# A hybrid decoder step on one core: a second buffer of values, rows' sums in the ring of general buffers, the state's chain over nine tenths of a pair's stretch, and the order at the program's two ends

## The chip, the cores and the metric

One core of a Trainium2 chip runs the whole program. The time is the device time of one execution in microseconds (us), the median of several; lower is better. In the profile the engines are PE (TensorE, matmuls), PEld (its weight loads), DVE (VectorE), ACT (ScalarE), POOL (GpSimd) and SP (SyncE, which issues nearly all DMAs).

## The reference

One layer of a hybrid decoder for a prompt of 2048 rows and 8 sequences of 4 new rows, all in float32 with a width of 1024. The normalised rows are multiplied by one large matrix; a short convolution, a recurrent state (RWKV-7, 16 heads of 64) and two gates work on its columns; two output projections are gated and added, a third follows, then a residual sum and a norm.

```python
h = _rmsnorm(x, norm_g)
p = jnp.einsum('bsd,dn->bsn', h, w_in)                 # 1024 x 10368 columns
...
y_c = bg * conv * jax.nn.silu(zc)                      # conv: 3 taps of cg * xin
...
# the state of a head, row after row:
S = (S * d_t[:, :, None, :] + sa[..., None] * (kk_t * a_t)[:, :, None, :]
     + v_t[..., None] * k_t[:, :, None, :])            # sa = S @ (-kk_t)
y = jnp.einsum('bhvk,bhk->bhv', S, r_t)
...
m = jax.nn.sigmoid(gc) * (y_c @ w_out_c) + jax.nn.sigmoid(gr) * (y_r @ w_out_r)
out = x + m @ w_o                                      # then the final _rmsnorm
```

The outputs are the normed rows and the new states of convolution, shift and recurrence.

## The kernel before

**Matrices in halves.** Every large product is made of float32 operands split into a high part and a low part (`fp32r`): a tile of rows stands in XH and XL, a tile of weights in whl[0] and whl[1], and three matmuls (high by high, low by high, high by low) give one product. Weights are read from HBM into `wraw`, ACT copies the high part (`w_advance`), DVE subtracts to get the low part (`w_lows`), and both halves are stored for later sets.

**Sets and pairs.** The 2048 rows are four sets of 512 (`th` 0 to 3; the last, LAST, has the 32 new rows as well), and in each set the 16 heads are 8 pairs (`p`). The main stream of PE is the projections (`ip<-XH,whl`, `ip<-XL,whl`) of nine or ten column blocks per pair. Around it runs, as side jobs written as Python generators (`Side`, line 498), the recurrence in chunks of 64 rows: `rwkv_keys` (decays, keys), `rwkv_solve` and `rwkv_merge` (scores GM and the inverse of a triangular matrix, Xbd), `rwkv_load` (values into SV, transposed keys into BKt), `rwkv_chain` and `rwkv_out` (norm of the rows' sums Yc, output).

**The chain** (line 1362) is what is serial. For each of the 8 chunks of a pair: PE multiplies the state (`pa<-S,AR`), DVE adds into UB, PE multiplies (`pb<-UB,Xbd`), ACT copies the upper half of SV, PE multiplies (`pb<-SV,BKt`), DVE makes the new state S. The chain of pair k runs during the stretch of pair k+1.

**What sets the order.** While the program is recorded, a planner (`Clock`) keeps a time per engine. `begin_pair` (1761) and `run_pair` (1775) give each side job a piece of the pair's stretch by the shares in CUTS, and `drive` (552) lets a job take its next step when its share and the operands' planned readiness allow. PE's order is that in which it is recorded; DVE's and ACT's instructions are sorted by planned start at the end (1825). Engines take their instructions in order. A DMA is booked by `dma_start` (336) on SP's clock with its size over 290 bytes per ns.

**Buffers.** `tmp` (605) is a ring of 8 general tiles (`Ring`, 182); if none is free, side jobs are run ahead until one is. SV and Yc exist once, so `rwkv_load` of a pair waits for the chain of the pair before (it writes SV and BKt), and the chain waits for the `rwkv_out` before it. During sets 1 to 3 the job `comb` makes sums of quarters of the output matrices: `part_of` (1584) copies a high half into one of two tiles `qs` (ACT), subtracts the low half (DVE) and stores both (SP, 512 KB), 108 times.

**The two ends.** At the start `prep_first` (741) scales the first rows (kept in GM), transposes them on PE and makes XH and XL. At the end `out_phase` (2063) adds the last product of each quarter of 128 rows to its sum (`out_done`, 2022), squares it, and `finish` (2009) makes the root (DVE, POOL, DVE) and scales both halves of the rows, quarter after quarter.

In the trace nearly all instructions have line L264 and the DMAs L337: there the recording layer calls the engine. So tiles tell them apart.

Of the kernel before, what the change touches and what calls it, by code (L numbers as in the profile page):

```python
# [30 lines left out]
CUTS = {"most": (0.7, 0.0, 0.0, 0.34, 0.7, 0.95, 0.95), "last": (0.6, 0.3, 0.68, 0.4, 0.7, 0.97, 0.9),  # L31
# [313 lines left out]
def hybrid_kernel(tc, x_prompt, x_sample, state_conv, state_shift, state_rwkv, norm_g, w_in, conv_w,  # L345
# [61 lines left out]
    raws, parts_, lows = {}, {}, []  # L407
    state = {"use": 0, "dma": 0, "split": 0}

    def w_advance(dma, split, load):  # L410
        while state["dma"] < min(dma, len(order)):
            _, src, n, _, there = order[state["dma"]]
            if not there:
                raw = wraw_p.tile()
                SP.dma_start(out=raw.rearrange("p (kt n) -> p kt n", n=n),
                             in_=src.rearrange("(kt p) n -> p kt n", p=P))
                raws[state["dma"]] = raw
            state["dma"] += 1
        while state["split"] < len(order):
            i = state["split"]  # L420
            _, src, n, keep, there = order[i]
            if i >= (load if there else split):
                break
            hl = whl_p.tile([P, 2, NB * P], F32R, name="whl")
            if there:
                for c0, c1, part in keep if isinstance(keep, list) else [(0, NB * P, keep)]:
                    SP.dma_start(out=hl.bitcast(F32)[:, :, c0:c1], in_=part)
            else:
                raw = raws.pop(i)
                A.copy(hl[:, 0], raw)  # L430
                lows.append((hl, raw, keep))
            parts_[i] = tuple(hl[:, k].rearrange("p (kt n) -> p kt n", n=n) for k in range(2))
            state["split"] += 1

    def w_lows():
        while lows:
            hl, raw, keep = lows.pop(0)
            was, clock.kind = clock.kind, "low"
            V.tensor_tensor(out=hl[:, 1], in0=raw, in1=hl[:, 0].bitcast(F32), op=ALU.subtract)
# [165 lines left out]
    tmp = Ring(ph1.enter_context(tc.tile_pool(name="tmp", bufs=1)), [P, NT + 64], 8, clock)  # L605
# [17 lines left out]
    SV = xp.tile([P, NC1, P], F32, name="SV")  # L623
# [5 lines left out]
    def load_early(i):  # L629
# [3 lines left out]
        else:  # L633
            xt = (BKt if i == 2 else SV).rearrange("p a b -> p (a b)")[:, 0:D]
# [106 lines left out]
    def prep_first(half):  # L741
# [4 lines left out]
        for k, i in enumerate(ts):  # L746
            xt = early[i]
            sc = rstd[:, i:i + 1]
            if k % 2:
                A.activation(out=xt, in_=xt, func=AF.Copy, scale=sc)  # L750
            else:
                V.tensor_scalar(out=xt, in0=xt, scalar1=sc, scalar2=None, op0=ALU.mult)
# [548 lines left out]
    def rwkv_load(th, p, o):  # L1301

        vT = o["vT"]
        samp = th == LAST
# [6 lines left out]
        yield W["bt"], (), 1  # L1311
        for c0 in range(0, NCH + samp, 4):
# [4 lines left out]
            if c0 == NCH:  # L1317
                T.transpose(pt[:, P:2 * P], vT[:, NTT[th] - P:NTT[th]], ident)
                A.copy(SV[64:64 + NSAMP, NCH, :], pt[P - NSAMP:P, P:2 * P])
            A.copy(BKt[:, c0:c0 + k, :], pt[:, 0:k * P].rearrange("p (c x) -> p c x", x=P))  # L1320
            yield W["bt"], (), 1
        yield W["merge"], [SV[64:128], BKt]
# [31 lines left out]
    def all_rows(o, GM, Yc, samp):  # L1354

        o["left"] = o.get("left", 1 + samp) - 1
        if not o["left"]:
            own_rows(0, NCH, GM, Yc)
            if samp:
                own_rows(NCH, 1, GM, Yc)  # L1360

    def rwkv_chain(th, p, o):
# [4 lines left out]
        S = St[p]  # L1367
# [41 lines left out]
    def rwkv_sequences(th, p, o):  # L1409
# [64 lines left out]
        yield W["samp"], [SV[0:64, c, :]], 2  # L1474
        all_rows(o, GM, Yc, True)

    def rwkv_out(th, p, o):
# [24 lines left out]
        for c2 in range(2):  # L1502
            for h in range(2):
# [3 lines left out]
                             func=AF.Identity, scale=lw[HS[c2], p:p + 1], bias=lb[HS[c2], p:p + 1])  # L1507
        if samp:
# [239 lines left out]
    def zero_rest():  # L1748
        for t in (UP[64:128, 1].bitcast(F32), UP[0:64, 3].bitcast(F32), BK[:, NCH], ARB[0][:, NCH], ARB[1][:, NCH], *XB, *UB, SV[:, NCH]):
# [11 lines left out]
    def begin_pair(th, p, total):  # L1761
# [10 lines left out]
        job["load", k] = Side(rwkv_load(th, p, o), "load", [job["keys", k]] + read(k - 1)).over(f[4], f[5])  # L1772
        return o

    def run_pair(th, p, total, end):
# [4 lines left out]
        after = [prior("merge", k), prior("load", k), prior("out", k - 1)]  # L1780
# [228 lines left out]
    def finish(r, pieces, m=P):  # L2009

        ms, f, z = (nwt.tile([P, 1], F32, name=f"f{i}", bufs=2)[0:m] for i in range(3))
        V.scalar_tensor_tensor(out=ms, in0=fs[0:m, 1, r:r + 1], scalar=1.0 / D, in1=fs[0:m, 0, r:r + 1], op0=ALU.mult, op1=ALU.add)
        G.tensor_tensor(out=f, in0=ms, in1=mhalf[0:m], op=ALU.pow)
        V.scalar_tensor_tensor(out=z, in0=f, scalar=ms, in1=f, op0=ALU.mult, op1=ALU.mult)
# [5 lines left out]
        SP.store(d0, t0)  # L2020

# [41 lines left out]
    def out_phase(n):  # L2063
# [8 lines left out]
        if n == len(seq) - 1:  # L2072
# [108 lines left out]
```

## Time and profile before

| | us |
|---|---|
| median of 3 runs | 3046.71 (3045.75 to 3051.43) |
| profiled execution, whole | 3049.82 |
| its span, first to last instruction | 3048.1 |
| PE busy in the span | 2986.7 |
| DVE busy | 2162.2 |
| ACT busy | 1346.4 |
| mean granted clock of PE | 0.997 |

The difference of 1.7 us between the profiled execution and its span lies outside the first and last instruction. A matmul's end is modelled in the trace and overlaps the next one's start, so PE's busy time hides short delays; the distance from start to start tells them. A wait is named by what ended it.

### The profile page before, as it was taken

Reading aid. Unit: us, or ns where it says so; the run is one execution under the profiler, and the core shown is the slowest. Engines: PE = TensorE matmul, PEld = TensorE weight load, DVE = VectorE, ACT = ScalarE, POOL = GpSimd, SP = SyncE. Lnnn points to the kernel's source line nnn. Section 1 sums busy time; section 2 is a strip of 40 time slices with the busy share of each in tenths; the row PEclk is TensorE's granted clock in tenths of the full one; section 3 lists DMA queues with packets and bytes.
Section 4 is the critical chain, followed back from the end, with each engine's and each line's share of the span. In section 5 each row is a group of like instructions: output and inputs, shape, how many; then the busy total and the mean of one; then the engine's idle time right before and its main releaser. Section 6 shows DMA issues by size and latency. Waiting matters only on the chain. (4 is left out here: it accounts for less than half of the span.)

```text
span 3048.1 us, 56138 instructions
## 1 busy us (share of the span) xinstructions
PE 2986.7 (98%) x21370; PEld 2559.5 (84%) x21370; DVE 2162.2 (71%) x5504; ACT 1346.4 (44%) x2745; POOL 314.2 (10%) x520
## 2 busy tenths in 40 slices
PE   7999999999999999999999999999999999999998
PEld 6778777788887788788787899999999998888996
DVE  5777777767777777777777777667767744486675
ACT  5555554554444445444444444444444322424223
POOL 2011111111111111111111110000100000000000
PEclk9999999999999999999999999999999999999999
DMA  7877767766666667666665665444344589998775
GB/s 273 291 235 238 252 223 236 230 222 227 207 218 210 212 215 246 219 218 218 218 223 208 201 214 181 150 136 143 128 141 135 169 262 330 325 325 294 267 261 195
DMA packets 319731, 678.05 MB, mean 222 GB/s; under 512 B 47610, under 2 KB 179827, under 8 KB 269798
## 3 DMA queue, kind: packets, MB, share of 16 engines
q1 hardware_dynamic: 310758, 670.27, 65.0%
q10 hardware_dynamic: 8704, 4.20, 0.5%
q8 instruction: 169, 2.77, 0.4%
q14 instruction: 100, 0.82, 0.1%
HBM read 479.10 MB, written 195.28 MB: 221 GB/s over the span
## 5 line engine op out<-in xcount | busy, mean ns | idle before, releaser
L264 PE MATMUL ip<-XH,whl 128*128 128x512 f32 (+3 forms) x6832 | 1854.3, 351 | 4.6 <-DVE whl L264 3.8
L264 PEld LDWEIGHTS ip<-XH,whl 128*128 128x128 f32 x6832 | 1173.9, 189 | 136.3 <-issue 7.0
L264 PE MATMUL ip<-XL,whl 128*128 128x512 f32 (+3 forms) x3416 | 1195.7, 350 | 2.2 <-POOL XL L264 2.2
L264 PEld LDWEIGHTS ip<-XL,whl 128*128 128x128 f32 x3416 | 646.6, 189 | 67.8 <-issue 5.5
L264 DVE SCALAR_TENSOR_TENSOR S<-pb,pe,sp 64x64 f32<-64x64 f32 x512 | 143.3, 280 | 98.2 <-PE pb L264 91.4
L264 DVE TENSOR_TENSOR tt<-Mi,X 128x60 f32<-128x60 f32 (+21 forms) x864 | 190.3, 220 | 24.9
L264 DVE TENSOR_TENSOR X<-X,tt 128x60 f32<-128x60 f32 (+21 forms) x864 | 187.9, 217 | 27.9
L264 ACT ACTIVATE sp<-S,pe 128x128 f32<-128x128 f32 x256 | 102.4, 400 | 205.8 <-DVE S L264 203.5
L264 ACT COPY SV<-pb 64x128 f32<-64x128 f32 x256 | 66.1, 258 | 283.8 <-PE pb L264 279.5
L264 DVE TENSOR_TENSOR UB<-pa,P 64x64 f32<-64x64 f32 x512 | 110.3, 215 | 111.8 <-PE pa L264 88.8
L264 ACT ACTIVATE tmp<-ip,vec 128x512 f32<-128x512 f32 (+2 forms) x174 | 103.0, 593 | 182.6 <-PE ip L264 178.0
L264 PE MATMUL acc<-XH,whl 128*128 128x264 f32 (+1 forms) x800 | 141.2, 329 | 0.5 <-DVE tmp L264 0.5
L264 PEld LDWEIGHTS acc<-XH,whl 128*128 128x128 f32 x800 | 119.0, 188 | 14.9 <-DVE tmp L264 0.7
L264 PEld LDWEIGHTS pb<-UB,Xbd 128*128 128x128 f32 x512 | 85.0, 188 | 40.5 <-PE ip L264 16.1
L264 PE MATMUL acc<-UA,whl 128*128 128x264 f32 (+1 forms) x720 | 116.1, 321 | 1.0 <-DVE My L264 1.0
L264 DVE TENSOR_TENSOR whl<-wraw,whl 128x1024 fp32r<-128x1024 f32 x81 | 101.8, 1256 | 20.5 <-ACT whl L264 19.8
L264 PEld LDWEIGHTS acc<-UA,whl 128*128 128x128 f32 x720 | 103.9, 188 | 12.1 <-DVE My L264 1.4
L264 PE MATMUL pb<-UB,Xbd 128*128 128x128 f32 x512 | 105.0, 287 | 8.3 <-DVE UB L264 7.2
L264 DVE TENSOR_TENSOR GM<-pt,mask_p 128x512 f32<-128x512 f32 x128 | 82.6, 686 | 42.9 <-PE pt L264 42.5
L264 PEld LDWEIGHTS pa<-S,AR 128*128 128x128 f32 x512 | 87.0, 189 | 26.8 <-DVE S L264 15.3
L264 PE MATMUL acc<-XL,whl 128*128 128x264 f32 (+1 forms) x616 | 108.6, 326 | 0.0
L264 PEld LDWEIGHTS pb<-SV,BKt 128*128 128x128 f32 x512 | 89.4, 188 | 20.4 <-ACT SV L264 6.4
(559 smaller groups left out, 4421.9 us busy)
## 6 DMA issues: line engine op xcount, KB each, us to landing
wraw<-in_w_in_dram SPq DMA_DIRECT2D x81, 512.0 KB
whl<-w_k SPq DMA_DIRECT2D x24, 1024.0 KB
whl<-w_r SPq DMA_DIRECT2D x24, 1024.0 KB
whl<-w_v SPq DMA_DIRECT2D x24, 1024.0 KB
whl<-w_z SPq DMA_DIRECT2D x24, 1024.0 KB
whl<-w_xin SPq DMA_DIRECT2D x24, 1024.0 KB
whl<-w_cg SPq DMA_DIRECT2D x24, 1024.0 KB
whl<-w_zc SPq DMA_DIRECT2D x24, 1024.0 KB
```

The costliest lines, as they stand in the source:

```text
L264: r = f(*a, **k)
```

## The change

It has four parts.

1. *Values in two buffers, sums in the ring.* SV becomes SVB[0] and SVB[1], used in turn in sets 0 to 2; the new rows' values stay in the last chunk of the first (SVS). The transposes that fill the values leave `rwkv_load` and are a job of their own, `rwkv_values`, at 0.5 to 0.75 of the stretch; `rwkv_load` (BKt alone) goes to 0.9 to 1.0. Yc of sets 0 to 2 is a tile of `tmp`, freed by `rwkv_out`; the ring gets a ninth tile. The chain no longer waits for the output of the pair before, but for that of the pair before it. In the last set Yc takes the place of SVB[1], and its cuts stay.
2. *The chain's stretch.* In CUTS "most", the chain's end goes from 0.7 to 0.9 and the output's end from 0.95 to 1.15.
3. *One buffer of halves.* `qs` has one tile instead of two.
4. *The ends.* The low parts of the first two weights are ordered behind the scaling of the first rows, the second weight's high part behind the scaling of the second. In the last product a quarter's sum and square come before the scaling of the quarter ahead.

```diff
+EARLY, TURN = (0.5, 0.75), (0.9, 1.0)
-CUTS = {"most": (0.7, 0.0, 0.0, 0.34, 0.7, 0.95, 0.95), "last": (0.6, 0.3, 0.68, 0.4, 0.7, 0.97, 0.9),
+CUTS = {"most": (0.9, 0.0, 0.0, 0.34, 0.7, 0.95, 1.15), "last": (0.6, 0.3, 0.68, 0.4, 0.7, 0.97, 0.9),
...
-    tmp = Ring(ph1.enter_context(tc.tile_pool(name="tmp", bufs=1)), [P, NT + 64], 8, clock)
+    tmp = Ring(ph1.enter_context(tc.tile_pool(name="tmp", bufs=1)), [P, NT + 64], 9, clock)
-    SV = xp.tile([P, NC1, P], F32, name="SV")
+    SVB = [xp.tile([P, NC1 - i, P], F32, name=f"SV{i}") for i in range(2)]
+    SVS = SVB[0][:, NCH, :]
...
-    def rwkv_load(th, p, o):
+    def rwkv_values(th, p, o):
 
         vT = o["vT"]
-        samp = th == LAST
+        SV = o["SV"] = SVB[(th * NB + p) % 2 if th < LAST else 0]
         yield 0.0, (), 1
         pt = new_pt([P, 512], F32, name="pt")
         for j in range(TPS):
             T.transpose(pt[:, j * P:(j + 1) * P], vT[:, j * P:(j + 1) * P], ident)
         for c2 in range(2):
             A.copy(SV[64:128, c2:NCH:2, :], pt[HS[c2]].rearrange("p (j x) -> p j x", x=P))
-        yield W["bt"], (), 1
+        yield W["bt"], [SV[64:128, 0:NCH]]
+
+    def rwkv_load(th, p, o):
...
-            o["Yc"] = rw.tile([P, NC1, 64], F32, name="Yc")[:, 0:NCH + (th == LAST)]
+            if th == LAST:
+                o["Yc"] = SVB[1].rearrange("p c x -> p (c x)")[:, 0:NC1 * 64].rearrange("p (c v) -> p c v", v=64)
+            else:
+                o["Yc"] = tmp.tile([P, TW], F32, name="tmp").rearrange("p (c v) -> p c v", v=64)[:, 0:NCH]
...
-    qs = [cb.tile([P, 2, 4 * P], F32R, name=f"qs{i}") for i in range(2)]
-    turns = [0]
+    qs = [cb.tile([P, 2, 4 * P], F32R, name="qs")]
 
     def part_of(w, key, j, src, scale=1.0):
 
-        hl = qs[turns[0] % 2]
-        turns[0] += 1
+        hl = qs[0]
...
-        job["load", k] = Side(rwkv_load(th, p, o), "load", [job["keys", k]] + read(k - 1)).over(f[4], f[5])
+        job["values", k] = Side(rwkv_values(th, p, o), "load", [job["keys", k]] + read(k - 1 - (th < LAST))).over(*((total * x for x in EARLY) if th < LAST else (f[4], f[5])))
+        job["load", k] = Side(rwkv_load(th, p, o), "load", [job["keys", k]] + read(k - 1)).over(*((f[4], f[5]) if th == LAST else (total * x for x in TURN)))
...
-        after = [prior("merge", k), prior("load", k), prior("out", k - 1)]
+        after = [prior("merge", k), prior("load", k), prior("values", k), prior("out", k - 1 - (th < LAST))]
...
+    for b in setup["lows"]:
+        behind_of(b, setup["scaled"][0])
+    behind_of(setup["casts"][1], setup["scaled"][1])
...
+    def last_done(d, k, j):
+
+        root = finish_root(rows_at("x2", j - 1)[0]) if j else None
+        added = None
+        if j < NP:
+            o = o_at(d, "x2", j)
+            added = V.tensor_tensor(out=o, in0=o, in1=acc[j][:, 0, :], op=ALU.add).ins
+            square(o, *rows_at("x2", j))
+        if j:
+            finish_rows(root, [(o_at(d, x, j - 1), x_rows(d, x, j - 1, y_prompt)) for x in ("x1", "x2")], added=added)
...
-                out_done(d, k, j)
+                last_done(d, k, j)
+            last_done(d, k, NP)
```

`finish_root` and `finish_rows` are the two halves of `finish`; `behind_of(b, a)` keeps b behind a on their engine. The changed program has one line more ahead of the recording layer, so its rows say L265.

**PE, the chain in the third set, fifth pair, second chunk** (S_451 is that pair's state, UB_221 and Xbd_218 the chain's operands, SV the values; ip the projections). Before:

```order
4927 L264 MATMUL pa<-S_451,AR_212 128x128
4928 L264 MATMUL pt<-ident,tmp 128x128 x4
4929 L264 MATMUL ip<-XL,whl 128x512
4930 L264 MATMUL ip<-XH,whl 128x512
4931 L264 MATMUL pb<-UB_221,Xbd_218 128x128
4932 L264 MATMUL ip<-XH,whl 128x512
4933 L264 MATMUL ip<-XL,whl 128x512
4934 L264 MATMUL ip<-XH,whl 128x512
4935 L264 MATMUL pb<-SV,BKt 128x128
```

Now, at the same chunk:

```order
4898 L265 MATMUL pa<-S_451,AR_212 128x128
4899 L265 MATMUL ip<-XH,whl 128x512 x2
4900 L265 MATMUL ip<-XL,whl 128x512
4901 L265 MATMUL ip<-XH,whl 128x512 x2
4902 L265 MATMUL ip<-XL,whl 128x512
4903 L265 MATMUL ip<-XH,whl 128x512 x2
4904 L265 MATMUL ip<-XL,whl 128x512
4905 L265 MATMUL ip<-XH,whl 128x512 x2
4906 L265 MATMUL pb<-UB_221,Xbd_218 128x128
4907 L265 MATMUL ip<-XL,whl 128x512
4908 L265 MATMUL ip<-XH,whl 128x512 x2
4909 L265 MATMUL pb<-SV_222,BKt 128x128
```

Eleven projection matmuls stand between the chunk's first and second step where two and a group of transposes stood; between second and third there are three in both.

**DVE at the start** (whl<-wraw,whl is the low part of a weight, nw and rstd the rows' statistic, GM the first rows, tmp<-ip,vec an evacuation of their transposes). Before:

```order
12 L264 TENSOR_TENSOR whl<-wraw,whl 128x1024
13 L264 TENSOR_TENSOR mask_s<-mask_p,seqm 128x32 x2
14 L264 STREAM_TRANSPOSE X_263<-tmp 128x256
15 L264 TENSOR_TENSOR nw_288<-rstd 128x2
16 L264 TENSOR_TENSOR whl<-wraw,whl 128x1024
17 L264 TENSOR_TENSOR nw_288<-nw_288,nw_285 128x2
18 L264 TENSOR_SCALAR nw_288<-nw_288 128x2
19 L264 TENSOR_TENSOR rstd<-rstd,nw_288 128x2
20 L264 TENSOR_SCALAR GM_217<-GM_217,rstd 128x1024
21 L264 TENSOR_TENSOR tmp<-ip,vec 128x512 x2
```

Now:

```order
12 L265 TENSOR_TENSOR mask_s<-mask_p,seqm 128x32 x2
13 L265 STREAM_TRANSPOSE X_264<-tmp 128x256
14 L265 TENSOR_TENSOR nw_289<-rstd 128x2
15 L265 TENSOR_TENSOR nw_289<-nw_289,nw_286 128x2
16 L265 TENSOR_SCALAR nw_289<-nw_289 128x2
17 L265 TENSOR_TENSOR rstd<-rstd,nw_289 128x2
18 L265 TENSOR_SCALAR GM_217<-GM_217,rstd 128x1024
19 L265 TENSOR_TENSOR whl<-wraw,whl 128x1024
20 L265 TENSOR_TENSOR tmp<-ip,vec 128x512
21 L265 TENSOR_TENSOR whl<-wraw,whl 128x1024
22 L265 TENSOR_TENSOR tmp<-ip,vec 128x512
```

Both low parts moved from ahead of the scaling of GM to behind it.

**DVE at the end** (Rx is a half of a quarter's rows, acc the last product, fs the sums of squares, f the steps of the root). The third and fourth quarter before:

```order
4833 L264 SCALAR_TENSOR_TENSOR f_33044<-fs 128x1
4834 L264 SCALAR_TENSOR_TENSOR f_33046<-f_33045,f_33044 128x1
4835 L264 SCALAR_TENSOR_TENSOR f_33045<-f_33046,f_33045 128x1
4836 L264 SCALAR_TENSOR_TENSOR Rx_29057<-Rx_29057,f_33045,fg 128x512
4837 L264 TENSOR_TENSOR Rx_29057<-Rx_29057,acc_29068 128x512
4838 L264 SCALAR_TENSOR_TENSOR f_33070<-fs 128x1
```

Now:

```order
4842 L265 SCALAR_TENSOR_TENSOR f_33048<-fs 128x1
4843 L265 TENSOR_TENSOR Rx_29049<-Rx_29049,acc_29060 128x512
4844 L265 SCALAR_TENSOR_TENSOR f_33050<-f_33049,f_33048 128x1
4845 L265 SCALAR_TENSOR_TENSOR f_33049<-f_33050,f_33049 128x1
4846 L265 SCALAR_TENSOR_TENSOR Rx_29049<-Rx_29049,f_33049,fg 128x512
4847 L265 SCALAR_TENSOR_TENSOR f_33062<-fs 128x1
```

The fourth quarter's sum stands three rows earlier, ahead of the rest of the third quarter's root and its scaling.

More of the change, by code (lines that the diff above doesn't have):

```diff
@@ L407, in hybrid_kernel @@
     raws, parts_, lows = {}, {}, []
+    setup = {"casts": [], "lows": [], "scaled": {}}
     state = {"use": 0, "dma": 0, "split": 0}
@@ L429, in w_advance @@
                 raw = raws.pop(i)
-                A.copy(hl[:, 0], raw)
+                r = A.copy(hl[:, 0], raw)
+                if i < 2:
+                    setup["casts"].append(r.ins)
                 lows.append((hl, raw, keep))
@@ L438, in w_lows @@
             was, clock.kind = clock.kind, "low"
-            V.tensor_tensor(out=hl[:, 1], in0=raw, in1=hl[:, 0].bitcast(F32), op=ALU.subtract)
+            r = V.tensor_tensor(out=hl[:, 1], in0=raw, in1=hl[:, 0].bitcast(F32), op=ALU.subtract)
+            if len(setup["lows"]) < 2:
+                setup["lows"].append(r.ins)
             clock.kind = was
@@ L633, in load_early @@
         else:
-            xt = (BKt if i == 2 else SV).rearrange("p a b -> p (a b)")[:, 0:D]
+            xt = (BKt if i == 2 else SVB[0]).rearrange("p a b -> p (a b)")[:, 0:D]
         SP.dma_start(out=xt, in_=x_prompt[0, i * P:(i + 1) * P, :])
@@ L749, in prep_first @@
             if k % 2:
-                A.activation(out=xt, in_=xt, func=AF.Copy, scale=sc)
+                r = A.activation(out=xt, in_=xt, func=AF.Copy, scale=sc)
             else:
-                V.tensor_scalar(out=xt, in0=xt, scalar1=sc, scalar2=None, op0=ALU.mult)
+                r = V.tensor_scalar(out=xt, in0=xt, scalar1=sc, scalar2=None, op0=ALU.mult)
+            setup["scaled"][i] = r.ins
         for q in range(NB // KG):
@@ L1333, in own_values @@
             for h in range(2):
-                T.matmul(pt[HS[h], i * 64:(i + 1) * 64], lhsT=GM[64:128, c0 + i, 0, h, :], rhs=SV[64:128, c0 + i, HS[h]],
+                T.matmul(pt[HS[h], i * 64:(i + 1) * 64], lhsT=GM[64:128, c0 + i, 0, h, :], rhs=chunk(o, c0 + i)[64:128, HS[h]],
                          start=True, stop=True)
@@ L1348, in own_rows @@
             for h in range(2):
-                T.matmul(pt[HS[h], i * 64:(i + 1) * 64], lhsT=GM[:, c0 + i, 1, h, :], rhs=SV[:, c0 + i, HS[h]],
+                T.matmul(pt[HS[h], i * 64:(i + 1) * 64], lhsT=GM[:, c0 + i, 1, h, :], rhs=chunk(o, c0 + i)[:, HS[h]],
                          start=True, stop=True)
@@ L1507, in rwkv_out @@
                              func=AF.Identity, scale=lw[HS[c2], p:p + 1], bias=lb[HS[c2], p:p + 1])
+        if not samp:
+            tmp.free(Yc)
         if samp:
@@ L1748, in zero_rest @@
     def zero_rest():
[L1749 removed]
+        for t in (UP[64:128, 1].bitcast(F32), UP[0:64, 3].bitcast(F32), BK[:, NCH], ARB[0][:, NCH], ARB[1][:, NCH], *XB, *UB, SVS):
             G.memset(t, 0.0)
@@ L2013, in finish, with finish_rows @@
         G.tensor_tensor(out=f, in0=ms, in1=mhalf[0:m], op=ALU.pow)
-        V.scalar_tensor_tensor(out=z, in0=f, scalar=ms, in1=f, op0=ALU.mult, op1=ALU.mult)
+        return ms, f, z
+    def finish_rows(root, pieces, m=P, added=None):
+        ms, f, z = root
+        r = V.scalar_tensor_tensor(out=z, in0=f, scalar=ms, in1=f, op0=ALU.mult, op1=ALU.mult)
+        if added:
+            behind_of(r.ins, added)
         V.scalar_tensor_tensor(out=f, in0=z, scalar=3.0, in1=f, op0=ALU.subtract, op1=ALU.mult)
```

41 lines of the change are left out of this document (25 added, 16 removed).

## The prediction

> **What bounds the kernel now.** The page comes first, for who is busy; then the busy time of each engine stage by stage; then who ended TensorE's idle time.
>
> ```profile
> span 3048.1 us, 56138 instructions
> PE 2986.7 (98%) x21370; PEld 2559.5 (84%) x21370; DVE 2162.2 (71%) x5504; ACT 1346.4 (44%) x2745; POOL 314.2 (10%) x520
> ```
>
> TensorE (PE) is drawn busy for all but 61.4 us, and the change removes and adds no matmul. So only its idle time, and small delays under the drawn matmuls, can move. The next rows are the stages: start, first blocks, sets 0 to 3 and, behind the last stage (2490 to 3038.7), the end. Columns: from:to, length, then busy time (and instructions) of PE, PEld, DVE, ACT, POOL, then clock and DMA.
>
> ```profile
> 0.00:13.58 13.58, 0.24 (x2) 0.18 (x2) 5.73 (x21) 8.17 (x11) 11.65 (x47) 1.00 0.70 236
> 13.58:30.00 16.42, 14.42 (x95) 13.07 (x96) 13.86 (x31) 9.37 (x15) 5.99 (x8) 1.00 0.86 305
> 30.00:650.00 620.00, 603.30 (x3968) 490.18 (x3968) 460.04 (x1137) 324.69 (x602) 73.62 (x116) 0.99 0.76 248
> 650.00:1220.00 570.00, 565.50 (x3956) 462.48 (x3956) 423.38 (x1169) 274.23 (x580) 73.63 (x122) 1.00 0.64 216
> 1220.00:1795.00 575.00, 570.23 (x4023) 469.59 (x4022) 434.56 (x1190) 272.35 (x579) 74.58 (x119) 1.00 0.63 214
> 1795.00:2490.00 695.00, 686.48 (x6204) 646.71 (x6203) 488.07 (x1498) 291.66 (x719) 59.49 (x91) 1.00 0.48 159
> 3038.70:3048.10 9.40, 0.02 (x1) 0.00 (x0) 3.23 (x10) 2.37 (x6) 1.10 (x2) 0.70 0.45 168
> ```
>
> Length less PE's busy time gives PE's idle time: 13.3 us before the first transposes, 2.0 in the first blocks, 16.7, 4.5 and 4.8 in sets 0, 1 and 2, 8.5 in set 3, 9.4 after the last matmul. The change reaches the first two, sets 0 to 2 and the end: some 51 us in all. Who ended PE's idle time from 30 to 1795 us (in total us, times, longest):
>
> ```profile
> PE pb L264 <- DVE UB L264: 6.4, 14, 1.3
> PE pt L264 <- DVE Mc L264: 3.9, 4, 1.7
> PE ip L264 <- DVE whl L264: 3.8, 5, 1.3
> PE pa L264 <- DVE S L264: 1.9, 5, 0.8
> PE pb L264 <- ACT SV L264: 1.6, 3, 1.0
> ```
>
> The state's chain (pa, pb<-UB, pb<-SV) waits 6.4 + 1.9 + 1.6 = 9.9 us in 22 waits; that is what a longer chain can win visibly.
>
> **The start.** DVE takes the split of two weights (whl) between the rows' statistic and the scaling of the first rows:
>
> ```profile
> 7.68 0.72 POOL L264 TENSOR_TENSOR rstd<-nw,mhalf 128x2 f32<-128x2 f32 x1 [0.48 <-DVE vec L264]
> 8.84 1.23 DVE L264 TENSOR_TENSOR whl<-wraw,whl 128x1024 fp32r<-128x1024 f32 x1 [1.26 <-ACT whl L264]
> 9.34 1.04 ACT L264 CAST whl<-wraw 128x1024 fp32r<-128x1024 f32 x1 [0.53 <-DMA wraw<-in_w_in_dram]
> 11.72 0.15 DVE L264 TENSOR_TENSOR nw<-nw,nw 128x2 f32<-128x2 f32 x1
> 12.33 1.19 DVE L264 TENSOR_SCALAR GM<-GM,rstd 128x1024 f32<-128x1024 f32 x1
> 12.33 1.15 ACT L264 ACTIVATE GM<-GM,rstd 128x1024 f32<-128x1024 f32 x1 [0.47 <-DVE rstd L264]
> 13.58 3.67 PE L264 MATMUL ip<-ident,GM 128*128 128x128 f32 x16 [10.78 <-DVE GM L264]
> 14.73 0.69 DVE L264 TENSOR_TENSOR tmp<-ip,vec 128x512 f32<-128x512 f32 x1 [1.21 <-PE ip L264]
> 17.62 0.76 PE L264 MATMUL ip<-XH,whl 128*128 128x256 f32 x2 [0.17 <-DVE tmp L264]
> ```
>
> POOL's power ends at 8.40. After it DVE needs one product and then the 0.61 us from 11.72 to 12.33; mask and transpose of setup fit into DVE's idle 1.26 us ahead. So the scaling can begin near 9.2, 3.1 us earlier, and the transposes near 10.4. The two splits do not vanish: 1.23 us each, they now stand among the four evacuations of the transposes, and the second also waits for ACT, whose second cast (1.04 us) now follows ACT's scaling (1.15): 9.2 + 1.15 + 1.04 = 11.4. On DVE, with 0.6 to 0.7 us for a product or low part: split to 11.6, product to 12.3, split to 13.5, product 14.2, low part 14.9, third product 15.5. The first projection needs that third product's bank, so it starts near 15.7 instead of 17.62: 1.9 us. Behind it the rows of tiles 2 and 3 come earlier by up to the 3.1. I take **-2.5**, bounds -1 (the third weight's load is not moved) and -3.1.
>
> **The end.** Each quarter's sum now goes to DVE before the scaling of the quarter ahead. Before:
>
> ```profile
> 3037.63 1.09 PE L264 MATMUL acc<-whl,XL 128*128 128x512 f32 x4
> 3039.76 0.41 DVE L264 SCALAR_TENSOR_TENSOR f<-f,f 128x1 f32<-128x1 f32 x2 [0.66 <-POOL f L264]
> 3040.88 0.68 DVE L264 TENSOR_TENSOR Rx<-Rx,acc 128x512 f32<-128x512 f32 x1
> 3042.40 0.16 DVE L264 SCALAR_TENSOR_TENSOR f<-fs 128x1 f32<-128x1 f32 x1 [0.85 <-ACT junk L264]
> 3043.68 0.75 DVE L264 SCALAR_TENSOR_TENSOR Rx<-Rx,f,fg 128x512 f32<-128x512 f32 x1
> ```
>
> The last matmul ends at 3038.72 and the last sum starts at 3040.88, behind the third quarter's scaling. In the new order it starts near 3039.05 and ends at 3039.75; the third quarter's scaling, 1.12 us (3039.76 to 3040.88), then runs beside ACT's square, to 3040.85. The last quarter's root then starts at 3040.85 instead of 3042.40, and what follows is unchanged: **-1.6**, bounds -1 and -1.8 (2.16 us would go if nothing came in between).
>
> **The chain.** One step, third set, fifth pair, second chunk, on PE, DVE and ACT:
>
> ```profile
> 1578.84 0.38 PE L264 MATMUL pa<-S,AR 128*128 128x128 f32 x2
> 1579.26 0.45 DVE L264 TENSOR_TENSOR UB<-pa,P 64x64 f32<-64x64 f32 x2
> 1579.96 0.38 PE L264 MATMUL pb<-UB,Xbd 128*128 128x128 f32 x2
> 1580.38 0.26 ACT L264 COPY SV<-pb 64x128 f32<-64x128 f32 x1 [0.97 <-PE pb L264]
> 1580.41 0.39 PE L264 MATMUL ip<-XL,whl 128*128 128x512 f32 x1
> 1580.64 0.40 PE L264 MATMUL ip<-XH,whl 128*128 128x512 f32 x1
> 1580.88 0.38 PE L264 MATMUL pb<-SV,BKt 128*128 128x128 f32 x2
> ```
>
> UB is ready at 1579.71 and PE takes it at 1579.96; SV at 1580.64, taken at 1580.88: a margin of 0.25 us each. PE takes its instructions in order, so DVE or ACT late by more than that stops the projections too. By the order lists, this chunk has 11 projection matmuls between pa and pb<-UB after, against two and four transposes before; over the 192 chunks of sets 0 to 2 the median stretch from pa to pb<-UB, weighed with 0.23 us a 512-column matmul, grows from 1.6 to 2.0 us, that from pb<-UB to pb<-SV from 0.7 to 1.3. That is 0.4 to 0.6 us more margin. The 22 visible waits average 0.45 us. A wait is drawn short, since a projection matmul is drawn about 0.4 us long but is followed after 0.23 (1580.41 to 1580.64): 0.17 us of each is hidden, so the 22 are worth 9.9 + 22 * 0.17 = 13.6 us. Some come back elsewhere, because DVE's work is the same (423.38 of 570 us in set 1), and after the change more than before of the stretches to pb<-UB are over 2.2 us (65 against 49), which is DVE planned late, not pacing. I take half: **-6.8**, bounds 0 and -13.6. PE is interrupted as often (1239 times before, 1238 after), so that costs nothing. The other waits of the list (Mc, whl: 7.7 us) come from DVE's order, drawn anew: 0, bounds -7 and +7. In set 3 the cuts are the same and the idle 8.5 us stays. The second values' buffer, its transposes (moved, not added) and the sums in the ring cost no instruction; the ring has nine buffers of which one or two hold sums, so seven or eight are left for what had eight. That is covered by planning ahead; if a buffer is missing, a side job is forced early: inside the +7.
>
> **The single buffer qs.** This is the part that can cost. Halves of split weights are made by ACT and DVE and stored 108 times; the next copy by ACT must now wait until the store has read the buffer.
>
> ```profile
> 1449.38 0.69 DVE L264 SCALAR_TENSOR_TENSOR qs<-q,qs 128x512 fp32r<-128x512 f32 x1
> 1449.76 0.61 ACT L264 ACTIVATE qs<-q 128x512 fp32r<-128x512 f32 x1
> 1450.14 0.56 SPq L337 DMA_DIRECT2D uo<-qs  x1
> 3044.85 0.38 SPq L337 DMA_DIRECT2D out_dram<-Rx  x1
> ```
>
> Here ACT copies the next part before DVE has even finished this one; with one buffer that copy moves behind the store. How long a store takes is seen at the program's end: 3.25 us from the issue of the last one (256 KB) to 3048.1, where these have 512 KB. The planner's table (dma_start) books 512 KB / 290 = 1.8 us, so ACT's copy can stand in its queue 1.45 us or more too early, and what is behind it waits. In ACT's new order the chain's SV copy is next or next but one after 35 of the 108 copies. Nothing: 0. All 35 late by 1.45 - 0.25: +42. A copy is due once in 11 us ((1877.9 - 679.8) / 107, from first to last start), so most stores have landed by then, and the margin at pb<-SV has doubled: I take 35 * 1/2 * 0.17 = **+3**, near the lower end.
>
> ```profile
> L264 ACT ACTIVATE qs<-q x108: 613/630/644, 679.8 to 1877.9; 128x512 fp32r<-128x512 f32 x108
> ```
>
> The Trainium skill, DMA: Bandwidth & Descriptors, "Anatomy of one DMA — SWDGE (gpsimd) path", speaks against a single buffer: every DMA pays about 2 us fixed, mostly the receipt of the last byte, plus bytes / 436 GB/s. By it 512 KB take an estimated 3.2 us, the copy stands 1.4 us early, and a quarter of the 108 delayed by that much would be +38 us. It is fitted to another issuing path; the 3.25 us of the row for half the bytes, beside other stores, is the bound kept above.
>
> **Sum.** -2.5 - 1.6 - 6.8 + 3 = -7.9 us. The profiled execution took 3049.8 us (span 3048.1), so 3041.9 for its like; the median of the runs shown is 3046.7, 3.1 lower, so **3039 us**.
>
> **Rivals.** (1) *The store's wait takes the place of the chain's*, the slower side. For it: in-order ACT, the 0.25 us margins. Against: 11 us between copies. It makes the kernel slower (over 3052.8) from 17 us on, half a microsecond at each of the 35 copies; at 0.7 us it is +24 with the other terms kept: 3046.7 - 10.9 + 24 = 3060. Chance 0.13. (2) *The spread doesn't spread what PE waits for*: waits are where DVE is late, and they stay. For it the 65 long stretches, against it the margins. Chain 0, start, end and store stay: 3046.7 - 1.1 = 3045.6. Chance 0.30. (3) *The slack pays everywhere*: chain -13.6, half of the other waits in sets 0 to 2 -7, start -3.1, end -1.6, store 0: 3021. For it set 0's 16.7 idle us against 4.5 in set 1; chance 0.12. Forecast: 0.45, by itself 3032 to 3046.
>
> **Range and chances.** A measurement of this kernel can tell about 0.2% (6 us) from no change: under 3040.6 is faster, over 3052.8 slower. Forecast 0.40 and rival 3 0.12 give faster 0.52; rival 2 and the rest of the forecast 0.35; rival 1 0.13. Rival 1 and the far half of rival 3 are left out: 3025 to 3053.
>
> **What would show it.** Start: the first GM scaling near 9.2, first projection near 15.7. End: last sum within 0.4 us of the last matmul. Chain: PE's waits for UB, S and SV from 30 to 1795 us near 5 instead of 9.9 us. Store: ACT idle before qs with a DMA as the one that ended it; if that exceeds 100 us and PE waits for SV more than before, rival 1 it is. Wrong it would be if PE's idle time in set 0 grew, or the ring forced side jobs.

## The result and the profile after

The changed kernel is **slower**: 3068.26 us (median of 5 runs, 3065.97 to 3072.51) against 3046.71, a ratio of 1.0069, 95% interval [1.0057, 1.0080]. The prediction had 3039 us, range 3025 to 3053: the wrong side. Its profiled execution has a span of 3066.2 us, 18.1 more than before.

The page of the kernel after begins so:

```profile
span 3066.2 us, 56128 instructions
PE 2985.2 (97%) x21370; PEld 2553.1 (83%) x21370; DVE 2170.2 (71%) x5504; ACT 1346.3 (44%) x2745; POOL 322.0 (11%) x520
```

TensorE is drawn busy 1.5 us less than before, so its idle time went from 61.4 to 81.0 us: in this execution the whole loss is drawn as waiting. The busy time by stage says where; the stages are cut where the same work begins, so their lengths differ a little from those of before (columns as there).

```profile
0.00:13.93 13.93, 0.24 (x1) 0.18 (x1) 6.91 (x19) 5.32 (x8) 11.21 (x47) 1.00 0.67 229
13.93:30.00 16.07, 13.33 (x77) 11.96 (x77) 14.52 (x26) 9.56 (x16) 5.29 (x6) 1.00 0.85 280
30.00:653.00 623.00, 600.91 (x3964) 489.36 (x3962) 462.21 (x1142) 328.09 (x605) 78.17 (x117) 1.00 0.76 248
653.00:1226.00 573.00, 562.18 (x3907) 458.23 (x3907) 423.54 (x1163) 270.50 (x574) 74.13 (x120) 1.00 0.63 213
1226.00:1808.00 582.00, 571.58 (x4089) 469.88 (x4087) 435.88 (x1201) 272.58 (x580) 77.37 (x118) 1.00 0.63 213
1808.00:2510.00 702.00, 691.36 (x6221) 647.60 (x6221) 491.55 (x1499) 295.33 (x725) 61.16 (x94) 1.00 0.48 158
3058.70:3066.20 7.50, 0.00 (x0) 0.00 (x0) 2.93 (x8) 2.06 (x4) 0.55 (x1) 0.64 0.54 204
```

Length less busy time: idle 22.1, 10.8, 10.4 and 10.6 us in sets 0 to 3, against 16.7, 4.5, 4.8 and 8.5 before. Only the end won, 9.4 to 7.5 us; its last sum starts at once when the last product is there:

```profile
3058.70 0.69 DVE L265 TENSOR_TENSOR Rx<-Rx,acc 128x512 f32<-128x512 f32 x1 [0.91 <-PE acc L265]
```

Who ended TensorE's idle time from 30 to 1808 us (total us, times, longest):

```profile
PE pa L265 <- DVE S L265: 10.3, 13, 1.6
PE pb L265 <- DVE UB L265: 9.0, 14, 2.7
PE pb L265 <- ACT SV L265: 5.7, 7, 1.3
PE pt L265 <- DVE Mc L265: 4.2, 6, 1.2
PE ip L265 <- DVE whl L265: 3.6, 3, 2.0
```

The three waits of the chain (the first three rows) were to fall from 9.9 to about 5 us; they are 25.0. And qs, in the view of that tile (idle time that a copy or low half ended, then who waited, in us and times):

```profile
  DMA uc<-qs: 16.1, 6
  DMA ucs<-qs: 15.9, 7
  ACT qs L265: 15.3, 14
  DMA uot<-qs: 12.9, 9
...
who waited for it (us, times):
  ACT qs L265: 83.3, 41
  DVE qs L265: 15.3, 14
```

ScalarE stood still in front of a store 41 times, 2.0 us each in the mean, which it never did before. One of them, on ScalarE and on SyncE's queue:

```profile
697.86 0.59 SPq L338 DMA_DIRECT2D uc<-qs  x1
698.40 0.40 ACT L265 ACTIVATE sp<-S,pe 128x128 f32<-128x128 f32 x1 [0.51 <-DVE S L265]
701.52 0.63 ACT L265 ACTIVATE qs<-q 128x512 fp32r<-128x512 f32 x1 [2.72 <-DMA uc<-qs]
702.18 0.26 ACT L265 COPY SV<-pb 64x128 f32<-64x128 f32 x1
```

The store is issued at 697.86 and the copy starts at 701.52: 3.66 us, where the planner books 1.8. Over all 41 stops the copy starts 3.1 to 7.8 us after the issue (counted over the rows). Here ScalarE stands still for 2.72 us, and the chain's SV copy stands behind.

The start, on VectorE and GpSimd, and TensorE's first projection; the first two rows are the same step and GpSimd's last zeros in the kernel before (L264):

```profile
11.88 1.79 POOL L264 MEMSET S<- 128x128 f32 x8
11.91 0.19 DVE L264 TENSOR_SCALAR nw<-nw 128x2 f32<-128x2 f32 x1
...
8.77 0.45 POOL L265 MEMSET UP<- 64x128 f32 x2
8.79 0.16 DVE L265 TENSOR_TENSOR nw<-nw,nw 128x2 f32<-128x2 f32 x1
8.99 4.16 DVE L265 TENSOR_SCALAR nw<-nw 128x2 f32<-128x2 f32 x1
...
12.04 1.25 POOL L265 MEMSET S<- 128x128 f32 x8
13.19 0.16 DVE L265 TENSOR_TENSOR rstd<-rstd,nw 128x2 f32<-128x2 f32 x1
13.38 0.75 DVE L265 TENSOR_SCALAR GM<-GM,rstd 128x1024 f32<-128x1024 f32 x1
19.11 0.77 PE L265 MATMUL ip<-XH,whl 128*128 128x256 f32 x2 [0.83 <-DVE tmp L265]
```

The statistic's steps do come early (8.79 instead of 11.72), but one of them, on 128x2 numbers, takes 4.16 us where it took 0.19: it begins just after GpSimd's run of zeros has begun (8.77) and ends at 13.15, as that run ends (13.29). The scaling begins at 13.38: 1.05 us later than before, not 3.1 earlier; the first projection at 19.11, 1.49 us later than before.

### The profile page after: what moved, and what is told of

It reads as the page before. It is cut to its first block, busy times and chain, and to the rows that moved or that the text cites. A ratio compares the mean times of both kernels' runs of the same rounds, so it can differ in the third digit from the quotient of the medians.

```text
span 3066.2 us, 56128 instructions
## 1 busy us (share of the span) xinstructions
PE 2985.2 (97%) x21370; PEld 2553.1 (83%) x21370; DVE 2170.2 (71%) x5504; ACT 1346.3 (44%) x2745; POOL 322.0 (11%) x520
## 5 line engine op out<-in xcount | busy, mean ns | idle before, releaser
L265 PE MATMUL ip<-XH,whl 128*128 128x512 f32 (+3 forms) x6832 | 1843.1, 350 | 5.3 <-DVE whl L265 3.6
L265 PEld LDWEIGHTS ip<-XH,whl 128*128 128x128 f32 x6832 | 1169.2, 189 | 133.6 <-issue 7.9
L265 PE MATMUL ip<-XL,whl 128*128 128x512 f32 (+3 forms) x3416 | 1196.5, 350 | 1.5 <-POOL XL L265 1.5
L265 PEld LDWEIGHTS ip<-XL,whl 128*128 128x128 f32 x3416 | 645.5, 189 | 68.2 <-issue 4.8
L265 DVE SCALAR_TENSOR_TENSOR S<-pb,pe,sp 64x64 f32<-64x64 f32 x512 | 142.9, 279 | 113.5 <-PE pb L265 103.0
L265 DVE TENSOR_TENSOR X<-X,tt 128x60 f32<-128x60 f32 (+21 forms) x864 | 188.6, 218 | 28.4
L265 DVE TENSOR_TENSOR tt<-Mi,X 128x60 f32<-128x60 f32 (+21 forms) x864 | 187.5, 217 | 25.0
L265 ACT ACTIVATE tmp<-ip,vec 128x512 f32<-128x512 f32 (+2 forms) x174 | 103.1, 593 | 178.1 <-PE ip L265 176.3
L265 ACT COPY SV<-pb 64x128 f32<-64x128 f32 x256 | 66.1, 258 | 259.1 <-PE pb L265 255.2
L265 ACT ACTIVATE sp<-S,pe 128x128 f32<-128x128 f32 x256 | 102.5, 400 | 173.5 <-DVE S L265 170.1
L265 DVE TENSOR_TENSOR UB<-pa,P 64x64 f32<-64x64 f32 x512 | 110.0, 215 | 74.5 <-PE pa L265 58.1
L265 PE MATMUL acc<-XH,whl 128*128 128x264 f32 (+1 forms) x800 | 141.2, 329 | 0.6 <-DVE tmp L265 0.5
L265 PEld LDWEIGHTS acc<-XH,whl 128*128 128x128 f32 x800 | 119.0, 188 | 15.3 <-DVE tmp L265 0.7
L265 DVE TENSOR_TENSOR GM<-pt,mask_p 128x512 f32<-128x512 f32 x128 | 82.6, 686 | 61.5 <-PE pt L265 61.2
L265 PEld LDWEIGHTS pb<-UB,Xbd 128*128 128x128 f32 x512 | 84.9, 188 | 46.8 <-PE ip L265 15.9
L265 PE MATMUL acc<-UA,whl 128*128 128x264 f32 (+1 forms) x720 | 116.1, 321 | 1.8 <-DMA whl<-w_gr 1.8
L265 PE MATMUL pb<-UB,Xbd 128*128 128x128 f32 x512 | 105.9, 288 | 12.3 <-DVE UB L265 10.8
L265 PEld LDWEIGHTS pa<-S,AR 128*128 128x128 f32 x512 | 87.2, 188 | 34.5 <-DVE S L265 23.2
L265 PEld LDWEIGHTS acc<-UA,whl 128*128 128x128 f32 x720 | 103.8, 188 | 13.2 <-issue 2.0
L265 DVE TENSOR_TENSOR whl<-wraw,whl 128x1024 fp32r<-128x1024 f32 x81 | 101.5, 1254 | 18.2 <-ACT whl L265 17.8
L265 PE MATMUL pa<-S,AR 128*128 128x128 f32 x512 | 102.3, 281 | 11.4 <-DVE S L265 11.3
L265 PEld LDWEIGHTS pb<-SV,BKt 128*128 128x128 f32 x512 | 88.9, 188 | 27.1 <-ACT SV L265 13.5
```

The source lines that it names most:

```text
L265: r = f(*a, **k)
```

## The experiments

Two theories stood at first. **A**: the single buffer's store holds ScalarE and what is queued there. **B**: the spread chain and its new order cost it. For the start **C**: GpSimd's zeros hold VectorE. All ratios are against the kernel before in the same session, whose median moved between 3046.3 and 3050.1 us, so they are compared by ratio; 0.001 is 3.0 us.

**One buffer alone.** In the kernel before:

```diff
-    qs = [cb.tile([P, 2, 4 * P], F32R, name=f"qs{i}") for i in range(2)]
+    qs = [cb.tile([P, 2, 4 * P], F32R, name="qs")]
...
```

> The kernel before with one thing of the change alone: a single buffer qs for the halves of the combined weights. Theory A (ScalarE, in order, stands in front of a store that has not yet read the buffer, and the chain's copies of SV and the evacuations behind it come late): 3055 to 3066 us, 8 to 19 us over before; ScalarE idle before qs with a DMA as the one that ended it 60 us or more in all, where before it is about 0; the loss lies between the start of set 1 (some 624 us) and 1880 us, set 0 unchanged. Theory B (the loss comes from the spread chain and its new order on VectorE): 3045 to 3050 us.

3060.16 us, 1.0046 [1.0034, 1.0059], 14 us. ScalarE waits for qs as in the kernel after:

```profile
who waited for it (us, times):
  ACT qs L264: 87.5, 40
  DVE qs L264: 16.1, 15
```

A holds, but not as the prediction priced it. (The planner answers the missing buffer with a new order, some 6200 of TensorE's 21370 places, so the 14 us hold that, too; a run below keeps the order.) Of the chain's waits only that for S grew clearly (1.9 to 4.2 us); that for SV went from 1.6 to 2.0, that for UB fell from 6.4 to 4.1. TensorE's idle time grew by 5.4 us and its drawn busy time by 4.9 (2991.6 against 2986.7): no single wait of TensorE carries the delay, and about half of it lies under drawn matmuls.

**Two buffers in the kernel after**, with the room from the ring, and its control.

```diff
-    tmp = Ring(ph1.enter_context(tc.tile_pool(name="tmp", bufs=1)), [P, NT + 64], 9, clock)
+    tmp = Ring(ph1.enter_context(tc.tile_pool(name="tmp", bufs=1)), [P, NT + 64], 7, clock)
-    qs = [cb.tile([P, 2, 4 * P], F32R, name="qs")]
+    qs = [cb.tile([P, 2, 4 * P], F32R, name=f"qs{i}") for i in range(2)]
...
```

> The kernel after with two buffers qs again, the room taken from the ring of temporaries (seven in place of nine). Theory A: most of the loss of sets 1 to 3 goes, 3049 to 3056 us, and TensorE's waits for SV from 30 to 1808 us fall from 5.7 to about 2 us. Theory B: 3062 us or more, waits for S and UB stay near 19 us. A ring of seven that is too small would show as new waits of TensorE for temporaries and would hide A.

> The kernel after with a ring of seven temporaries in place of nine, single qs kept: the control of the run with two buffers and a ring of seven (3066). If that run gained nothing because the ring of seven took what the second buffer gave: 3076 to 3084 us here. If the second buffer is worth nothing in this order: 3065 to 3070.

With two buffers 3066.29 us (1.0059 [1.0046, 1.0073]), in theory B's range and 10 us over A's, with one 3082.96 (1.0111 [1.0097, 1.0125]). Taken alone the first would have spoken against A; its control shows that the ring of seven costs 0.0042 over after (13 us) and the second buffer wins 0.0052 (16 us).

**The start and the end alone**, and the same with the zeros moved.

```diff
+            zeros.append(G.memset(t, 0.0).ins)
...
+    for b in zeros:
+        behind_of(b, setup["carry"][2])
```

> The kernel before with the start's and the end's reordering alone. Theory C (GpSimd's run of memsets holds VectorE's tensor_scalar of the statistic back until it ends, near 13.2 us): first scaling near 13.4, first projection near 19.1, so +1.5 at the start and -1.9 at the end: 3045 to 3048 us. Rival (the start's loss in the changed kernel came from its other parts): scaling near 9.2, 3041 to 3043 us.

> As the run with the ends alone, and GpSimd's run of memsets (zeros that nothing needs before about 59 us) put behind its third copy of a carry, near 41 us. Theory C: the statistic's tensor_scalar takes 0.2 us, first scaling near 9.2, first projection near 15.7 to 16.2, 1.5 to 1.9 us earlier than before; with the end 3042 to 3044 us, faster than both kernels. Rival (the 4.16 us are not the memsets' doing): the scaling stays near 13.4 and the time is that of the ends alone within 1 us.

The ends alone: 3048.03 us, 0.9995 [0.9987, 1.0004]. The statistic's step is held there, too:

```profile
8.75 3.13 DVE L264 TENSOR_SCALAR nw<-nw 128x2 f32<-128x2 f32 x1
```

It ends at 11.88, just after the last eight zeros (S) have begun (11.80 to 13.59). With the zeros later: 3045.31 us, 0.9985 [0.9976, 0.9994], **4.6 us faster than before (by the interval 1.8 to 7.3) and the fastest kernel of this study**. The expected 3042 to 3044 was missed by 1.3 us. Its start, VectorE and TensorE:

```profile
8.81 0.17 DVE L264 TENSOR_SCALAR nw<-nw 128x2 f32<-128x2 f32 x1
9.02 0.16 DVE L264 TENSOR_TENSOR rstd<-rstd,nw 128x2 f32<-128x2 f32 x1
9.21 0.75 DVE L264 TENSOR_SCALAR GM<-GM,rstd 128x1024 f32<-128x1024 f32 x1
10.02 3.68 PE L264 MATMUL ip<-ident,GM 128*128 128x128 f32 x16 [7.32 <-DVE GM L264]
14.94 0.47 PE L264 MATMUL ip<-XH,whl 128*128 128x256 f32 x2 [0.76 <-DVE tmp L264]
```

C holds: VectorE's and ScalarE's orders are the same in both runs, GpSimd's differs, and the step is 0.17 us again.

**The wait for the store taken away in the kernel after's own order.** The stores read rows of an input weight in place of qs.

```diff
...
-        SP.store(units[w][key][j // 2][:, :, j % 2 * 4 * P:(j % 2 + 1) * 4 * P], hl.bitcast(F32))
+        dst = units[w][key][j // 2][:, :, j % 2 * 4 * P:(j % 2 + 1) * 4 * P]
+        SP.store(dst, hl.bitcast(F32), real=(dst, w_out_c[0][0:P, 0:8 * P].rearrange("p (k n) -> p k n", k=2)))
```

(`real` is what the DMA is given; the planner still books qs as the source.)

> The kernel after, but the 108 stores of qs read rows of an input weight instead of qs: the same bytes to the same places, planned as before, so nearly the same order on every engine (57 of ScalarE's 2306 rows differ), but no copy waits for a store any more. What is left out: the stored halves are not the split weights. Theory A (the wait of ScalarE for the store costs most in sets 1 to 3): 3053 to 3059 us, 10 to 15 less than after, ScalarE's idle time before qs that a DMA ends falls from 83 us to about 0. Theory B (the spread chain and its order cost it): 3064 us or more. Both at once (each costs about half): 3059 to 3063.

3057.3 us, 1.0028 [1.0017, 1.0039]. ScalarE's waits before qs are gone (0.9 us, one time). So the store's wait is worth 0.0069 - 0.0028 = 0.0041, 12.5 us, and 0.0028 - (-0.0005), 10 us, are left that neither it nor the ends explain. One more thing differs in this run: with nothing to wait for, the stores run ahead, the first at 142.8 us in place of 697.9 and the last at 854.8 in place of 1901.3, so that from 1226 to 1808 us the DMA engines are busy for 0.49 of the time in place of 0.63. So the 12.5 us are those of the wait and of the moved stores together. There TensorE still waits in the chain:

```profile
PE pa L265 <- DVE S L265: 8.9, 12, 1.6
PE pb L265 <- DVE UB L265: 7.6, 11, 3.5
...
PE pb L265 <- ACT SV L265: 3.1, 3, 1.6
```

**One number of the planner.** Still one buffer, everything computed:

```diff
-        c.add("SP", [out], [in_], size / 290.0, 2000.0)
+        at = c.add("SP", [out], [in_], size / 290.0, 2000.0)
+        if in_.tensor.name.startswith("qs"):
+            for e in c._hits(in_):
+                e[5] = max(e[5], at + 4000.0)
```

> The kernel after with one number of the planner changed: qs is booked as read 4.0 us after the store's planned start, in place of 1.8, so that the next copy is put later in ScalarE's order; still a single buffer. Theory A (the copy stands too early in an in-order queue and holds what is behind it): ScalarE's idle time before qs ended by a DMA falls from 83 us to under 35, and the time to 3057 to 3062. Theory B: 3065 us or more, whatever ScalarE's idle time does.

3058.18 us, 1.0026 [1.0017, 1.0035]; ScalarE's waits for qs fall from 83.3 to 20.1 us. An honest booking, with the stores in their places, wins as much (0.0043) as taking the wait away (0.0041). So a second buffer is not the only remedy: a copy put where its buffer is really free does as well. (The order is drawn anew here, too.)

**The old cuts, with the new places of loading.**

```diff
-CUTS = {"most": (0.9, 0.0, 0.0, 0.34, 0.7, 0.95, 1.15), ...
+CUTS = {"most": (0.7, 0.0, 0.0, 0.34, 0.7, 0.95, 0.95), ...
```

> The kernel after with the two old cuts of a pair again (chain over 0.7 of the stretch, output at 0.95); both values' buffers, the sums in the ring and the single qs stay. Theory B: the spread's price goes and the single buffer's stays, 3056 to 3062 us (the single buffer alone took 3060), TensorE's waits for S, UB and SV from 30 to 1808 us fall from 25 to about 12 us. Theory A alone: 3065 us or more.

> As the run whose stores read an input weight (3057.3), with the old cuts for the chain (0.7) and the output (0.95) but the new, late places for loading values (0.5 to 0.75) and keys (0.9 to 1.0). What is left out: the stored halves are not the split weights. It tells which half of the spread costs: beside the run with all old places (3049.8). Theory C (the chain's length, so that its last chunks meet the next pair's solve and its first the output): 3049 to 3052 us. Theory T (the keys' load squeezed into the last tenth, ahead of the next chain's first chunk): 3056 us or more; and then the 3083 of the run with the old cuts and a real store is this plus the store's wait.

With the real store 3083.06 us (3073.37 to 3091.38), 1.0107 [1.0088, 1.0126]: far over theory B's range, inside theory A's open one (3065 or more), and over the kernel after itself. ScalarE stands 111.9 us before qs there. Without the store's wait the same cuts give 3058.78, 1.0038 [1.0024, 1.0052]. So the same missing buffer costs 12 us in one order and 21 in another, and with the old length of the chain the kernel is no faster than with the new (1.0038 against 1.0028): the length alone is not the price. No run has the new length with the old places of loading, so what it costs by itself was not measured.

**What of the spread costs.** All without the store's wait, each a change of a few numbers to the run above that has it away (its stores running ahead in all of them):

> As the run whose stores read an input weight (3057.3), with the low half made in place of the high half, and in the room so won a tenth temporary in the ring. What is left out: the stored halves are not the split weights. It asks whether the sums kept in the ring make temporaries short. Theory R (they do): 3049 to 3053 us. Rival (nine are enough, 30 of ScalarE's rows move): 3056 to 3058.5.

> As the run whose stores read an input weight (3057.3), with one cut changed: a pair's output is due from 0.9 to 1.0 of the stretch instead of 0.9 to 1.15, so that it no longer runs beside the second chunk of the next pair's chain. What is left out: the stored halves are not the split weights. Theory O (the output's work on VectorE and ScalarE makes the second chunk's waits, 9.9 us against 2.4 before): these fall to about 3 us and the time to 3050 to 3053. Rival (they come from the keys of the pair after, due in the same place): waits and time unchanged within 2 us, or worse, since the output is squeezed.

> As the run whose stores read an input weight (3057.3), with all cuts of before: chain over 0.7 of the stretch, output to 0.95, values and keys loaded from 0.7 to 0.95. The two values' buffers, the sums in the ring and nine temporaries stay. What is left out: the stored halves are not the split weights. Theory S (the spread itself costs the 9 us that the waits for the store don't explain): 3047 to 3050 us, that of the ends alone. Theory L (the new places of buffers and sums cost them): 3055 us or more.

```diff
-EARLY, TURN = (0.5, 0.75), (0.9, 1.0)
+EARLY, TURN = (0.7, 0.95), (0.7, 0.95)
-CUTS = {"most": (0.9, 0.0, 0.0, 0.34, 0.7, 0.95, 1.15), ...
+CUTS = {"most": (0.7, 0.0, 0.0, 0.34, 0.7, 0.95, 0.95), ...
```

A tenth temporary: 3054.54, 1.0018 [1.0010, 1.0027]; output ended at the edge: 3054.93, 1.0019 [1.0010, 1.0028]. Both lie between the two forecasts and within the interval of the run that they start from, so neither is told apart from nothing. With all old places: 3049.83, **1.0002 [0.9993, 1.0010]**, not told apart from the ends alone. So the two values' buffers and the sums in the ring cost nothing that shows, and the new places cost 0.0026, 8 us. Which of them?

> As the run with stores that read an input weight and all old places (3049.8), with the keys' load alone at its new place, 0.9 to 1.0 of the stretch. What is left out: the stored halves are not the split weights. If the late load of the keys is the price: 3055 to 3060 us. If the values' early load is: 3047 to 3051.

> As the run with stores that read an input weight and all old places (3049.8), with the values' load alone at its new place, 0.5 to 0.75 of the stretch. What is left out: the stored halves are not the split weights. If the late load of the keys is the price: 3047 to 3051 us. If the values' early load is: 3055 to 3060. If both this and the run with the keys late lie near 3053, it is the order drawn anew that costs and neither place.

3057.55 (1.0032 [1.0020, 1.0043]) and 3056.01 (1.0024 [1.0015, 1.0034]): either move alone costs what all together do. Each time lies in the range in which the run's own move was to be the price, and neither near 3053, the mark set for the order. Prices that don't add up do not belong to one place. Each of these numbers makes the planner draw thousands of rows anew, and the chain's rows show different waits each time: S in the first (6.7 us), SV in the second (7.3).

> The kernel after, everything computed, with all old places, the store of qs booked as read after 4.0 us, and the zeros put behind the third carry; single qs, two values' buffers and the sums in the ring stay. If the store's wait, the places of loading and the zeros are all that cost: 3049.8 + 1 for what is left of the store's wait - 3 for the zeros, 3045 to 3049 us. If more is hidden in the layout: 3053 or more.

3051.84 us, 1.0015 [1.0006, 1.0024], some 3 us over its upper bound: ScalarE still waits 23.4 us for the stores of qs and VectorE 17.1 for ScalarE's copies, in an order that was once more another.

## Why the prediction was wrong

The terms in us, by the ratios (times 3046.7) where a run isolates them:

| step | forecast | measured |
|---|---|---|
| start and end together | -4.1 | -1.5 (interval -4.0 to +1.2) |
| of it the start | -2.5 | +1.5 (profile, kernel after) |
| of it the end | -1.6 | -1.9 (profile) |
| chain and other waits | -6.8 | +10, of which 8 the new places |
| single buffer | +3 | +12.5 |
| sum | -7.9 | +21 |

The chain's and the buffer's terms are differences between ratios, each uncertain by 4 to 5 us.

**The end** was right in mechanism and size: the last sum starts at 3058.70, at once behind the last matmul.

**The start** failed at "So the scaling can begin near 9.2", because each VectorE step was priced by its duration in the old order. With the zeros out of the way the steps hold: 9.21, and the first projection at 14.94 where 15.7 was forecast. What had been missed stands in the rows of before: the run of zeros (POOL 11.65 of the first 13.58 us busy) covers the stretch into which the step is moved; before, the step came at 11.91, beside the last zeros, and got through in 0.19 us (no run shows why it did there), and the scaling behind it took 1.19 us against 0.75 once they are gone. The Trainium skill, SBUF — State Buffer, "Who interferes with whom", says that VectorE's tensor_scalar can take a port pair shared with GpSimd and then fully blocks or is blocked, while tensor_tensor is held only by a GpSimd instruction that reads. The rows agree: tensor_scalar stood 4.16 us beside memsets, the tensor_tensor whl<-wraw,whl took 1.23 us beside the same memsets in the kernel before. The page speaks of the whole instruction; here the step sat out many in a row.

**The single buffer** was the right mechanism (rival 1) with the wrong size, in two factors. "I take 35 * 1/2 * 0.17" counted only copies with the chain's SV behind them, and only 0.17 us for each; the kernel after shows 41 stops of 2.0 us on ScalarE, and what they delay is mostly not SV: with the single buffer alone TensorE's wait for SV grew by 0.4 of some 14 us. And "a copy is due once in 11 us, so most stores have landed by then" measured from copy to copy. The low half and the store's issue lie in between (a median of 7.1 us before, counted over the 108 rows), so that in the kernel before 61 of the 107 next copies started less than 3.66 us after the issue of the store ahead. Its trace had this. The bounds 0 to +42 held. The rival's own signs came close: 83.3 us of ScalarE's standing against the 100 set for it, and SV's wait up from 1.6 to 5.7. The rule of the Trainium skill that was weighed there, DMA: Bandwidth & Descriptors, "Anatomy of one DMA — SWDGE (gpsimd) path" (2 us and bytes / 436 GB/s, an estimated 3.2 us), is nearer to the 3.66 us shown than the planner's 1.8. The +38 drawn from it was too much: 83.3 us of ScalarE's standing cost 12.5 us. The stores also reach into set 3, whose idle time was to stay at 8.5 us and became 10.6.

**The chain** failed at "that is 0.4 to 0.6 us more margin". More projections between two links are no margin when the link's own work is late: VectorE, too, takes its instructions in order, and its work was spread with the chain. Around the longest wait for S in the kernel after, VectorE and then TensorE:

```profile
1207.27 1.21 DVE L265 TENSOR_TENSOR X<-X,tt 128x72 f32<-128x72 f32 x1
1208.51 0.23 DVE L265 TENSOR_TENSOR tt<-Mi,X 128x68 f32<-128x68 f32 x1
...
1209.71 0.68 DVE L265 SCALAR_TENSOR_TENSOR qs<-q,qs 128x512 fp32r<-128x512 f32 x1
1210.31 0.23 DVE L265 TENSOR_TENSOR tt<-Mi,X 128x75 f32<-128x75 f32 x1
1210.57 0.24 DVE L265 TENSOR_TENSOR X<-X,tt 128x75 f32<-128x75 f32 x1
1210.73 0.57 DVE L265 SCALAR_TENSOR_TENSOR S<-pb,pe,sp 64x64 f32<-64x64 f32 x2
1211.36 0.49 PE L265 MATMUL pa<-S,AR 128*128 128x128 f32 x2 [1.59 <-DVE S L265]
```

The state's update stands behind the next pair's solve (X, tt), one step of which took 1.21 us instead of 0.23. Counted over the trace's rows, in none of the 13 waits for S from 30 to 1808 us was VectorE idle just before the update: it stood in VectorE's own queue, in 10 of them right behind such steps. And TensorE had 2.0 to 7.2 us of other work between pb<-SV and the wait, over 4 us in nine of the 13, so that half a microsecond more could not cover it. What made these waits more is not shown: the solve's steps stood right ahead in 4 of the 5 waits before, too, and ahead of 37 of 188 updates before and 41 after. Rival 2 had named this ("waits are where DVE is late") but let it cost nothing. It grew where no store can be blamed, too: "Wrong it would be if PE's idle time in set 0 grew", and it did, 16.7 to 22.1 us. By length it lost little: from the first projection (17.62 before, 19.11 after) to the last transpose of the next rows (638.57, 640.15) it took 621.0 us in both (the new order may have moved that transpose a little), but in the kernel before the stretch from 500 to 520 us had a granted clock of 0.83, against 1.00 after, an estimated 3.4 us (0.17 of 20). So in set 0 the spread won nothing.

What stays **open**: how the new places become 8 us. The chain's waits tell little of it: they are 19.6 us without the store's wait, but 15.8 with all old places as well (UB 7.3, S 5.5, SV 3.0), where nothing is lost, and the run with the old chain and late loads has only 10.4 and is no faster. There TensorE is drawn busy 14.9 us longer (2993.0 against 2978.1) at nearly the same idle time as with all old places. Of these an estimated 6 us are the granted clock of the two profiled executions, 0.997 against 0.999. The clock has a part in the medians, too: over the 94 runs of the kernel before beside the experiments, a mean granted clock lower by 0.001 goes with a time longer by 2.4 us. In the mean of the runs it was 0.9966 with the new places (0.9967 for the kernel before in that session) and 0.9978 with the old ones (0.9972), an estimated 2 of the 8 us. That the order drawn anew costs the rest, rather than a place, is argued from prices that don't add; it isn't shown.

## What to carry to other kernels

Before a buffer is taken away, compare what the planner books for its release with the trace's time from issue to release (here 1.8 against 3.1 us and more): an in-order engine pays the difference with everything that stands behind, and one honest number gave back as much as taking the wait away. Price a moved step by what runs on the other engines at its new place, not by its duration at the old one. A stretched chain gives slack only if the engine that makes each link has less in front of it.

## What the runs showed of the hardware that was not expected

A VectorE tensor_scalar on 128x2 numbers took 4.16 and 3.13 us beside a run of GpSimd's memsets, and 0.17 us with these moved; it was held over a row of memsets, not over one. Between the last, shorter zeros of the kernel before it took 0.19 us. Longer holds of about 1 us are rare in the sets: of the 1728 solve steps (X<-X,tt and tt<-Mi,X) six took 1.08 to 1.33 us instead of about 0.23, each while GpSimd had a tensor_tensor, as at 1207.27; in the kernel before there were seven.

A dip of TensorE's granted clock can belong to a place in the order: the stretch from 500 to 520 us has a granted clock of 0.83 in the kernel before and with the ends alone, and with the zeros later, where the work comes some 4 us earlier, the stretch from 496 to 516 us has it; in the kernel after, with another order, 500 to 520 us has 1.00. These are one execution each.
